# Attention's outputs divided once a pair, with the divisors and the last pair's outputs in slots kept up to the middle of the output projection

## The chip, the cores and the metric

The kernel runs on one core of a Trainium2 chip. The metric is device time in microseconds (us). The core has five engines with queues of their own: PE (TensorE, the matrix multiplier), DVE (VectorE), ACT (ScalarE), POOL (GpSimd) and SP (SyncE, which here only issues DMAs). Each works through its instructions in the order in which they were put, and waits on semaphores for the others. The time before is the median of three runs, 1177.61 us (1175.17 to 1178.79).

## The reference, cut to what matters

One layer of a hybrid block on x of shape (1, 1024, 1024), all in float32: an RMSNorm, one input projection split among three token mixers (causal pooling, gated linear attention, forgetting attention), the output projection of their concatenation with a residual, and a SwiGLU feed-forward with a residual and a last norm. The change is in the forgetting attention, 8 heads of width 64 over 1024 tokens:

```
s = einsum('bhqd,bhkd->bhqk', qb, kh) + Fb[..., None] - F[:, :, None, :]
s = where(kpos <= qpos, s, -inf)
p = softmax(s, axis=-1)
o = einsum('bhqk,bhkd->bhqd', p, vh)
```

The softmax divides each row of exponentials by its sum. Since the product with vh is linear in p, the division of row q may be done on p, ahead of the product, or on row q of o, behind it.

## The kernel before, in words

**Precision.** Matmuls that need float32's accuracy are made of three products of a rounded high part and a low remainder (names end in h and l, or hi and lo); a "split" makes the two parts, the high one by an ACT copy, the low one by a subtraction on DVE or POOL.

**Slots.** Nearly all of SBUF is 33 slots of 128 x 1024 floats plus 17 more in five rings. G(name) takes the first slot of the list idle, free(...) appends slots to its end (lines 50 to 58): first in, first out. A tile that inherits a slot waits until the last reader of the slot's tile before it is done. So which earlier tile a tile inherits from decides when its DMA may start. The rings join the list behind the attention (line 713).

**Order.** The program is written as one stream; a scheduler then fixes each engine's order ahead of the run, on its own model of durations, ahead in the program before later where both are ready. Hence projections that come later in the program fill PE between an attention item's steps.

**Stages.** The first norm, linear attention and pooling come first. Then, for four pairs of heads p (line 680): fox_attend (attention of the pair), fox_qk(p + 1) (the next pair's queries and keys, tiles q, k, kl, from the transposed input hT, the names zq and zk), then keep_mix(4 + p), which splits the pair's output y (tile mh is the high part) and stores both parts by two SP DMAs to a DRAM buffer mixs. For pair 1, fox_values also makes the values v2, v3 of the last two pairs.

fox_attend runs eight items (head a of the pair, group m of 256 queries: lines 634, 635). An item makes for both of its 128-query blocks the scores in PSUM (s, lines 576 to 579), adds the forget bias and takes the row minimum on DVE (line 581), and takes the exponential on ACT with the row sum as accumulated output (line 585). Then it takes the reciprocals of the two sums (line 588), and multiplies the first block's exponentials by them on POOL (line 591) and the second's on DVE (line 593). Blocks of four 128 x 128 tiles are then transposed on PE (pt, line 602), split by ACT and DVE (lines 604, 605), and multiplied with the values into o (line 616), which has one PSUM bank. Lines 619 and 622 add the two halves of o to the 64 output rows of head a: into tile y for pairs 0 to 2; for pair 3, whose order of items is m = 1, 0, 3, 2, into a temporary that is split at once into last_mix (lines 625, 626).

**Output projection.** It runs in two passes over eight token tiles of 128. The first pass (pxa, lines 699 to 708) takes the mixers 0 to 3: weights wo0 to wo3 (each in two slots, from the DRAM buffer wod), the input tile xa, and the mixes of 512 tokens at a time (mix0_g to mix3_g), 24 matmuls of 128x512 a tile. The second pass (pxb, line 935 on) takes mixers 4 to 7, that is the four pairs, with wo4 to wo7, mix4 to mix6 from DRAM and last_mix in place, and is followed a tile at a time by the second norm (norm2) and the first parts of the feed-forward (products named m, line 775).

Of the kernel before, what the change touches and what calls it, by code (L numbers as in the profile page):

```python
# [18 lines left out]
P = 128  # L19
# [12 lines left out]
def tile_hybrid_block(ctx: ExitStack, tc, x, w_fv, w_gv, w_zt, w_o, w_gu, w_down, ln, w_pool, w_a3, chans, b_f, consts, out):  # L32
    nc = tc.nc
    ACT, DVE, POOL, PE, SP = nc.scalar, nc.vector, nc.gpsimd, nc.tensor, nc.sync
# [4 lines left out]
    dpool = ctx.enter_context(tc.tile_pool(name="dp", bufs=1, space=bass.MemoryType.DRAM))  # L39
# [10 lines left out]
    def G(name, dtype=F32):  # L50
        i = idle.pop(0)
        t_ = big.tile([P, 1024], dtype, tag=f"g{i}", name=name)
        where[name] = i
        return t_

    def free(*names):
        for n in names:
            idle.append(where.pop(n))

    def R(name, dtype=F32, tag="p"):  # L60

# [50 lines left out]
    def PS(tag, name):  # L112
        return pst.tile([P, 512], F32, tag=tag, name=name, bufs=BANKS[tag])
# [22 lines left out]
    def half(name, dtype=F32):  # L136
        return rng.tile([P, 512], dtype, tag="tmp", name=name, bufs=2)
# [25 lines left out]
    def names_T(name):  # L163
        return [f"{name}{k}_{c}_{h}" for k in range(4) for c in range(2) for h in range(2)]
# [128 lines left out]
    last_mix = []  # L293
# [253 lines left out]
                    POOL.tensor_copy(t_[a][own[1 - a], csl], f(t_[a][own[a], csl]))  # L547
        return Q, K, KL

    def fox_item(p, a, m, ops, fb, V, Y):  # L550

        Q, K, KL = (t_[a] for t_ in ops)
        nm = f"{p}_{a}_{m}"
        rows = slice(64 * a, 64 * a + 64)
        Pb, Ws = [], []
        l, rl = S(f"l{nm}", 2), S(f"rl{nm}", 2)
        for i in range(2):
            qb = 2 * m + i
            W = P * (qb + 1)
            nh = 1 if W <= 512 else 2  # L560
            w = W // nh
            qs = slice(qb * P, (qb + 1) * P)
            mn = S(f"mn{nm}_{i}")
            if m >= 2:
                pb = R(f"pb{nm}_{i}")
            elif i == 0:
                pb2 = R(f"pb{nm}")
                pb = pb2[:, 0:512]
            else:
                pb = pb2[:, 512:1024]  # L570
            top = 3.0e38
            for h in range(nh):
                s = PS("s", f"s{nm}_{i}_{h}")
                ks = slice(h * w, (h + 1) * w)
                last = h == nh - 1
                PE.matmul(s[:, 0:w], Q[:, qs], K[:, ks], start=True, stop=False)  # L576
                PE.matmul(s[:, 0:w], Q[:, qs], KL[:, ks], start=False, stop=not last)  # L577
                if last:
                    PE.matmul(s[:, w - P:w], identr, maskr, start=False, stop=True)
# [5 lines left out]
            ACT.activation(pb[:, 0:W], pb[:, 0:W], AF.Exp, bias=mn[:, 0:1], scale=-1.0, accum_out=l[:, i:i + 1])  # L585
            Pb.append(pb)
            Ws.append(W)
        DVE.reciprocal(rl, l)  # L588
        for i, (pb, W) in enumerate(zip(Pb, Ws)):
            if i == 0:  # L590
                POOL.tensor_tensor(out=pb[:, 0:W], in0=pb[:, 0:W], in1=rl[:, 0:1].broadcast_to([P, W]), op=ALU.mult)  # L591
            else:
                DVE.tensor_scalar(out=pb[:, 0:W], in0=pb[:, 0:W], scalar1=rl[:, 1:2], scalar2=None, op0=ALU.mult)
        o = PS("o", f"o{nm}")
        for n in range(m + 1):
            pt = PS("pt", f"pt{nm}_{n}")
            pp = R(f"pp{nm}_{n}", F32R, tag="pp")
            cut = P if n == m else 0
            for b in range(2):
                for i in range(b if cut else 0, 2):  # L600
                    o0 = 256 * b + P * i - cut * b
                    PE.transpose(pt[:, o0:o0 + P], Pb[i][:, (2 * n + b) * P:(2 * n + b + 1) * P], ident)  # L602
            w = 512 - cut
            ACT.activation(pp[:, 0:w], pt[:, 0:w], AF.Copy)  # L604
            DVE.tensor_tensor(out=pp[:, 512:512 + w], in0=pt[:, 0:w], in1=f(pp[:, 0:w]), op=ALU.subtract)  # L605
            for b in range(2):
                kb = 2 * n + b
                o0 = cut * b
                v_ = V[p % 2][kb // 4][:, kb % 4, a]
                ph = pp[:, 256 * b:512 - o0] if b else pp[:, 0:256]  # L610
                pl = pp[:, 768:1024 - o0] if b else pp[:, 512:768]
                both = (o[:, o0:256], v_.rearrange("p s e -> p (s e)"), ph)
                high = (o[0:64, o0:256], v_[:, 0], pl)
                last = kb == 2 * m + 1
                for n_, args in enumerate((high, both) if last else (both, high)):
                    PE.matmul(*args, start=(kb == 0 and n_ == 0), stop=(last and n_ == 1))  # L616
        tmp = half(f"ot{nm}")
        ot, oy = tmp[0:64, 0:256], tmp[:, 256:512]
        ACT.activation(ot, o[64:128, 0:256], AF.Copy)
        if p < 3:  # L620
            oy = Y[:, m * 256:(m + 1) * 256]
        DVE.tensor_tensor(out=oy[rows], in0=o[0:64, 0:256], in1=ot, op=ALU.add)
        if p == 3:
            hi, lo = (last_mix[m // 2][rows, h, (m % 2) * 256:(m % 2 + 1) * 256] for h in range(2))
            ACT.activation(hi, oy[rows], AF.Copy)
            POOL.tensor_tensor(out=lo, in0=oy[rows], in1=f(hi), op=ALU.subtract)

    def fox_attend(p, ops, V, Y):
        fbs = []
        for a in range(2):  # L630
            fb = R(f"fb{p}_{a}", tag="fb")
            SP.dma_start(fb, Fd[2 * p + a:2 * p + a + 1, :].broadcast_to([P, T]))
            fbs.append(fb)
        for a, m in ([(a, m) for a in range(2) for m in range(4)] if p < 3 else [(a, m) for m in (1, 0, 3, 2) for a in range(2)]):
            fox_item(p, a, m, ops, fbs[a], V, Y)


    x3d = [dpool.tile([P, D], F32, name=f"x3d{tb}") for tb in range(NT)]
# [36 lines left out]
    V = fox_values(0, (B.within(1), o_[0][:1], o_[0][1:], o_[1][:1], o_[1][1:] + B.turned(0), B.turned(1), (), ()))  # L675
    for k in range(8):
        keep_wo(k)
    ops = fox_qk(0)
    free("gv0", "gv1", "attb0", "attb1")
    for p in range(4):  # L680
        if p == 3:
            last_mix += [G(f"mix7_{g}", F32R).rearrange("p (h t) -> p h t", h=2) for g in range(2)]
        Y = G(f"y{p}") if p < 3 else None
        fox_attend(p, ops, V, Y)
        done = [f"{n}{p}_{a}" for n in ("q", "k", "kl") for a in range(2)] + [f"v{p}_{i}" for i in range(2)]
        if p == 1:
            V = fox_values(1)
            free(*[done.pop() for _ in range(2)])
        if p < 3:
            ops = fox_qk(p + 1)  # L690
        if p == 2:
            free(*names_T("hT"))
        if p < 3:
            free(*done)
            keep_mix(4 + p, Y)
            free(f"y{p}")


    ws = [fetch_wo(k) for k in range(4)]
# [1 line left out]
    for g in range(2):  # L701
# [282 lines left out]
    sums = {}  # L984
# [139 lines left out]
```

## Time and profile before

| what | us |
|---|---|
| median of three runs | 1177.61 |
| lowest, highest | 1175.17, 1178.79 |
| profiled execution: its own time | 1177.97 |
| profiled execution: span of the core | 1176.0 |
| PE busy in the span | 1136.7 |
| DVE, ACT, POOL busy in the span | 823.9, 537.0, 339.7 |
| mean granted TensorE clock | 0.992 |
| last output of pair 0, 1, 2, 3 (start of the sum, line 622) | 300.0, 353.3, 435.5, 495.5 |
| first and last matmul of pxa | 398.1, 469.2 |
| first and last matmul of pxb | 470.5, 533.0 |

Times inside the span count from its start. PE's busy time is modelled from pipelined matmuls, so a stretch in which it is fully busy may still hold short waits. "<-" behind an idle time names what ended it. A row of the grouped views gives line, engine, operation, the tile written and those read, shape, count, then busy us, mean ns of one, and idle us ahead.

### The profile page before, as it was taken

The page shows a single profiled execution, that of the slowest core. Times are in us where ns is not written, and L with a number is a line of the kernel's source. Part 1 is how long each engine was busy: PE and PEld are TensorE (multiplying, and loading weights), DVE is VectorE, ACT ScalarE, POOL GpSimd, SP SyncE. Part 2 cuts the span into 40 slices and gives each one's busy share as a digit, 9 for nine tenths or more (in the row PEclk, how much of TensorE's full clock was granted, in tenths as well). Part 3 has the DMA queues.
Part 4 walks back from the last instruction along what each step waited for, and adds up shares of the span by engine and source line. Part 5 has one row for each costly group of instructions (what it writes and reads, how often), then busy time and mean ns, then how long its engine had stood idle before and what let it go on. Part 6 is the DMA issues. An engine that isn't in the chain of part 4 may idle for free.

```text
span 1176.0 us, 15954 instructions
## 1 busy us (share of the span) xinstructions
PE 1136.7 (97%) x5928; PEld 959.4 (82%) x5928; DVE 823.9 (70%) x1365; ACT 537.0 (46%) x972; POOL 339.7 (29%) x260
## 2 busy tenths in 40 slices
PE   6999998999999999998999999999999999999996
PEld 6877878889978888886888888888888888888885
DVE  7596364287746866579997768777776684976686
ACT  6453344366654644456453434443343344334344
POOL 2131122443322313110202221022202271660693
PEclk9999999999999999999999999999999999999999
DMA  7111179311203734431333232332324688333233
GB/s 250 36 37 37 37 264 351 102 37 37 91 18 122 308 127 158 163 127 37 107 100 134 88 128 69 119 121 95 109 80 152 215 323 291 107 96 105 80 118 143
DMA packets 57692, 150.45 MB, mean 128 GB/s; under 512 B 5080, under 2 KB 5512, under 8 KB 57616
## 3 DMA queue, kind: packets, MB, share of 16 engines
q1 hardware_dynamic: 57184, 147.87, 36.8%
q0 software_dynamic: 432, 1.57, 0.4%
q8 instruction: 46, 0.75, 0.3%
q14 instruction: 30, 0.25, 0.1%
HBM read 105.09 MB, written 44.34 MB: 127 GB/s over the span
## 4 chain that ended last, share of the span: by engine, by line
PE 81%; DVE 7%; DMA 5%; POOL 3%; issue 2%; ACT 1%; SPq 0%; POOLq 0%; ACTq 0%; DVEq 0%
PE m L775 35%; PE d L1031 13%; PE pxa L144 4%; PE pxb L144 3%; PE o L616 3%; PE psv L152 2%; PE pt L602 2%; POOL rw L873 2%; PE s L576 1%; PE s L577 1%; PE zq3p L152 1%; PE psg L144 1%; PE zgk1p L152 1%; PE zgg0p L152 1%; PE zq2p L152 1%
## 5 line engine op out<-in xcount | busy, mean ns | idle before, releaser
L775 PE MATMUL m<-hA_0h,wr 128*128 128x512 f32 x616 | 214.2, 391 | 0.9 <-ACT hr L730 0.9
L775 PE MATMUL m<-hA_1h,wr 128*128 128x512 f32 x616 | 214.6, 389 | 0.0
L775 PEld LDWEIGHTS m<-hA_0h,wr 128*128 128x128 f32 x616 | 116.0, 188 | 25.3 <-ACT hr L730 1.4
L775 PEld LDWEIGHTS m<-hA_1h,wr 128*128 128x128 f32 x616 | 115.7, 188 | 23.9
L757 ACT ACTIVATE wr<-ws 128x512 fp32r<-128x512 f32 x110 | 69.2, 631 | 120.6 <-DVE ws L756 61.9
L775 PE MATMUL m<-hA_0l,wr 128*128 128x512 f32 x308 | 120.2, 390 | 0.7 <-DVE hA_0l L905 0.7
L1031 PE MATMUL d<-lw,ha 128*128 128x512 f32 x308 | 119.8, 389 | 0.0
L775 PE MATMUL m<-hA_1l,wr 128*128 128x512 f32 x308 | 119.8, 389 | 0.0
L1031 PE MATMUL d<-hw,ha 128*128 128x512 f32 x308 | 119.3, 389 | 0.0
L1031 PE MATMUL d<-hw,la 128*128 128x512 f32 x308 | 118.4, 389 | 0.0
L827 POOL TENSOR_TENSOR cg<-cu,cu 128x512 f32<-128x512 f32 x11 | 19.7, 1793 | 304.9 <-DVE cu L804 268.6
L758 DVE TENSOR_TENSOR wr<-ws,wr 128x512 fp32r<-128x512 f32 x110 | 75.6, 694 | 26.9 <-ACT wr L757 26.8
L881 DVE TENSOR_TENSOR la<-ra,ha 128x1024 fp32r<-128x1024 f32 (+1 forms) x42 | 57.5, 1375 | 30.1 <-ACT ha L880 22.4
L873 POOL TENSOR_TENSOR rw<-wd,wd 128x512 f32<-128x512 f32 x33 | 59.6, 1833 | 48.0 <-PE d L1031 47.9
L591 POOL TENSOR_TENSOR pb<-pb,rl 128x128 f32<-128x128 f32 (+3 forms) x32 | 39.3, 1232 | 115.2 <-DVE rl L588 105.1
L880 ACT ACTIVATE ha<-ra 128x1024 fp32r<-128x1024 f32 (+1 forms) x42 | 41.2, 987 | 65.6 <-DMA ra<-cd 60.6
L775 PEld LDWEIGHTS m<-hA_0l,wr 128*128 128x128 f32 x308 | 58.0, 188 | 13.2 <-DVE hA_0l L905 1.1
L585 ACT ACTIVATE pb<-pb,mn 128x128 f32<-128x128 f32 (+3 forms) x64 | 49.5, 774 | 41.1 <-DVE mn L581 39.8
L605 DVE TENSOR_TENSOR pp<-pt,pp 128x512 fp32r<-128x512 f32 (+1 forms) x80 | 50.1, 631 | 25.7 <-ACT pp L604 25.5
L775 PEld LDWEIGHTS m<-hA_1l,wr 128*128 128x128 f32 x308 | 57.8, 188 | 12.1
L1031 PEld LDWEIGHTS d<-hw,ha 128*128 128x128 f32 x308 | 57.8, 188 | 12.1
L1031 PEld LDWEIGHTS d<-hw,la 128*128 128x128 f32 x308 | 57.8, 188 | 12.1
(399 smaller groups left out, 2699.1 us busy)
## 6 DMA issues: line engine op xcount, KB each, us to landing
ra<-cd SPq DMA_DIRECT2D x35, 512.0 KB, 3.9
wu<-in_w_gu_dram SPq DMA_DIRECT2D x22, 512.0 KB, 4.8
wg<-in_w_gu_dram SPq DMA_DIRECT2D x22, 512.0 KB, 3.7
wd<-in_w_down_dram SPq DMA_DIRECT2D x22, 512.0 KB, 6.7
mix<-mixs SPq DMA_DIRECT2D x14, 512.0 KB, 6.1
cd<-cg SPq DMA_DIRECT2D x11, 512.0 KB, 6.4
cd<-cs SPq DMA_DIRECT2D x11, 512.0 KB, 3.4
cd<-cu SPq DMA_DIRECT2D x11, 512.0 KB, 3.4
```

Of the source, the lines that this page charges most:

```text
L144: PE.matmul(ps, a, b, start=(n == 0), stop=(n == last))
L152: PE.matmul(ps, a, b, start=(i == 0 and n == 0), stop=(i == len(terms) - 1 and n == 2))
L585: ACT.activation(pb[:, 0:W], pb[:, 0:W], AF.Exp, bias=mn[:, 0:1], scale=-1.0, accum_out=l[:, i:i + 1])
L591: POOL.tensor_tensor(out=pb[:, 0:W], in0=pb[:, 0:W], in1=rl[:, 0:1].broadcast_to([P, W]), op=ALU.mult)
L605: DVE.tensor_tensor(out=pp[:, 512:512 + w], in0=pt[:, 0:w], in1=f(pp[:, 0:w]), op=ALU.subtract)
L757: ACT.activation(hi, src, AF.Copy)
L758: DVE.tensor_tensor(out=lo, in0=src, in1=f(hi), op=ALU.subtract)
L775: PE.matmul(ps, a, b, start=(n == 0), stop=(n == 11))
L873: POOL.tensor_tensor(out=raw_[:, j * 512:j * 512 + 512], in0=wd[h0, j0 + j][:, e0, :], in1=wd[h1, j0 + j][:, e1, :], op=op)
L880: ACT.activation(hi[:, sl], src, AF.Copy)
L881: DVE.tensor_tensor(out=lo[:, sl], in0=src, in1=f(hi[:, sl]), op=ALU.subtract)
L1031: PE.matmul(banks[t], a[:, o], b[:, ns], start=(j0 + j == 0 and m == 0), stop=(j0 + j == NF // 2 - 1 and m == 2))
```

## The change

The multiplications on the exponentials and the reciprocal of each item go away: an item now works on undivided exponentials, and ACT puts each row sum into one column of a tile of 16 columns for the pair. The new function divide(p, Y, sums, g) works on half g of the tokens (512), for both heads: it takes the reciprocals of 8 columns, transposes them on PE into 8 rows, copies these out of PSUM, writes them to a DRAM buffer Ld, reads them back twice as a broadcast over 64 partitions (one for each head), and multiplies Y by the result on POOL. All three DMAs are issued by POOL.

For pairs 0 to 2 both halves are divided behind fox_qk(p + 1), ahead of keep_mix. For pair 3 the first half is divided behind its fourth item and the second behind its last, and divide makes the split into last_mix for the half. So pair 3 now has a tile y3 as well. Each divide takes a slot rb. Those of pairs 0 to 2 are freed with y behind keep_mix; y3, rb3_0 and rb3_1 are freed behind the first pass of the output projection.

```diff
-        l, rl = S(f"l{nm}", 2), S(f"rl{nm}", 2)
...
-            ACT.activation(pb[:, 0:W], pb[:, 0:W], AF.Exp, bias=mn[:, 0:1], scale=-1.0, accum_out=l[:, i:i + 1])
+            ACT.activation(pb[:, 0:W], pb[:, 0:W], AF.Exp, bias=mn[:, 0:1], scale=-1.0, accum_out=sums[:, col(a, qb)])
...
-        DVE.reciprocal(rl, l)
-        for i, (pb, W) in enumerate(zip(Pb, Ws)):
-            if i == 0:
-                POOL.tensor_tensor(out=pb[:, 0:W], in0=pb[:, 0:W], in1=rl[:, 0:1].broadcast_to([P, W]), op=ALU.mult)
-            else:
-                DVE.tensor_scalar(out=pb[:, 0:W], in0=pb[:, 0:W], scalar1=rl[:, 1:2], scalar2=None, op0=ALU.mult)
...
-        if p < 3:
-            oy = Y[:, m * 256:(m + 1) * 256]
-        DVE.tensor_tensor(out=oy[rows], in0=o[0:64, 0:256], in1=ot, op=ALU.add)
+        DVE.tensor_tensor(out=Y[rows, m * 256:(m + 1) * 256], in0=o[0:64, 0:256], in1=ot, op=ALU.add)
+    Ld = dpool.tile([4, 2, 2, 512], F32, name="Ld")
+    def col(a, qb):
+        c = 8 * (qb // 4) + 4 * a + qb % 4
+        return slice(c, c + 1)
+    def divide(p, Y, sums, g):
+        nm = f"{p}_{g}"
+        rw = G(f"rb{nm}")
+        rl, rt, rb, gs = S(f"rl{nm}", 8), rw[0:8, 512:640], rw[:, 0:512], slice(g * 512, g * 512 + 512)
+        DVE.reciprocal(rl, sums[:, 8 * g:8 * g + 8])
+        pt = PS("pt", f"ptl{nm}")
+        PE.transpose(pt[0:8, 0:P], rl, ident)
+        ACT.activation(rt, pt[0:8, 0:P], AF.Copy)
+        POOL.dma_start(Ld[p, g].rearrange("a (q t) -> (a q) t", t=P), rt)
+        for a in range(2):
+            POOL.dma_start(rb[64 * a:64 * a + 64, :], Ld[p, g, a:a + 1, :].broadcast_to([64, 512]))
+        POOL.tensor_tensor(out=Y[:, gs], in0=Y[:, gs], in1=rb, op=ALU.mult)
         if p == 3:
-            hi, lo = (last_mix[m // 2][rows, h, (m % 2) * 256:(m % 2 + 1) * 256] for h in range(2))
-            ACT.activation(hi, oy[rows], AF.Copy)
-            POOL.tensor_tensor(out=lo, in0=oy[rows], in1=f(hi), op=ALU.subtract)
+            ACT.activation(last_mix[g][:, 0], Y[:, gs], AF.Copy)
+            POOL.tensor_tensor(out=last_mix[g][:, 1], in0=Y[:, gs], in1=f(last_mix[g][:, 0]), op=ALU.subtract)
...
-            fox_item(p, a, m, ops, fbs[a], V, Y)
+            fox_item(p, a, m, ops, fbs[a], V, Y, sums)
+            if p == 3 and (a, m) == (1, 0):
+                divide(p, Y, sums, 0)
+        if p == 3:
+            divide(p, Y, sums, 1)
...
-        Y = G(f"y{p}") if p < 3 else None
+        Y = G(f"y{p}")
...
+            for g in range(2):
+                divide(p, Y, sums, g)
             keep_mix(4 + p, Y)
-            free(f"y{p}")
+            free(f"y{p}", f"rb{p}_0", f"rb{p}_1")
...
-    free(*[f"wo{k}{h}" for k in range(4) for h in "hl"], *done)
+    free(*[f"wo{k}{h}" for k in range(4) for h in "hl"], *done, "y3", "rb3_0", "rb3_1")
```

More of the change, by code (lines that the diff above doesn't have):

```diff
@@ L548, in fox_qk, with fox_item @@
         return Q, K, KL
-    def fox_item(p, a, m, ops, fb, V, Y):
+    def fox_item(p, a, m, ops, fb, V, Y, sums):
         Q, K, KL = (t_[a] for t_ in ops)
@@ L554, in fox_item @@
         rows = slice(64 * a, 64 * a + 64)
-        Pb, Ws = [], []
-        l, rl = S(f"l{nm}", 2), S(f"rl{nm}", 2)
+        Pb = []
         for i in range(2):
@@ L583, in fox_item @@
                 top = t_[:, 0:1]
-            ACT.activation(pb[:, 0:W], pb[:, 0:W], AF.Exp, bias=mn[:, 0:1], scale=-1.0, accum_out=l[:, i:i + 1])
+            ACT.activation(pb[:, 0:W], pb[:, 0:W], AF.Exp, bias=mn[:, 0:1], scale=-1.0, accum_out=sums[:, col(a, qb)])
             Pb.append(pb)
-            Ws.append(W)
-        DVE.reciprocal(rl, l)
-        for i, (pb, W) in enumerate(zip(Pb, Ws)):
-            if i == 0:
-                POOL.tensor_tensor(out=pb[:, 0:W], in0=pb[:, 0:W], in1=rl[:, 0:1].broadcast_to([P, W]), op=ALU.mult)
-            else:
-                DVE.tensor_scalar(out=pb[:, 0:W], in0=pb[:, 0:W], scalar1=rl[:, 1:2], scalar2=None, op0=ALU.mult)
         o = PS("o", f"o{nm}")
@@ L616, in fox_item @@
                     PE.matmul(*args, start=(kb == 0 and n_ == 0), stop=(last and n_ == 1))
-        tmp = half(f"ot{nm}")
-        ot, oy = tmp[0:64, 0:256], tmp[:, 256:512]
+        ot = half(f"ot{nm}")[0:64, 0:256]
         ACT.activation(ot, o[64:128, 0:256], AF.Copy)
-        if p < 3:
-            oy = Y[:, m * 256:(m + 1) * 256]
-        DVE.tensor_tensor(out=oy[rows], in0=o[0:64, 0:256], in1=ot, op=ALU.add)
+        DVE.tensor_tensor(out=Y[rows, m * 256:(m + 1) * 256], in0=o[0:64, 0:256], in1=ot, op=ALU.add)
[15 more added lines that the diff above has]
+        POOL.tensor_tensor(out=Y[:, gs], in0=Y[:, gs], in1=rb, op=ALU.mult)
         if p == 3:
-            hi, lo = (last_mix[m // 2][rows, h, (m % 2) * 256:(m % 2 + 1) * 256] for h in range(2))
-            ACT.activation(hi, oy[rows], AF.Copy)
-            POOL.tensor_tensor(out=lo, in0=oy[rows], in1=f(hi), op=ALU.subtract)
+            ACT.activation(last_mix[g][:, 0], Y[:, gs], AF.Copy)
+            POOL.tensor_tensor(out=last_mix[g][:, 1], in0=Y[:, gs], in1=f(last_mix[g][:, 0]), op=ALU.subtract)
     def fox_attend(p, ops, V, Y):
@@ L633, in fox_attend @@
             fbs.append(fb)
+        sums = S(f"l{p}", 16)
         for a, m in ([(a, m) for a in range(2) for m in range(4)] if p < 3 else [(a, m) for m in (1, 0, 3, 2) for a in range(2)]):
-            fox_item(p, a, m, ops, fbs[a], V, Y)
+            fox_item(p, a, m, ops, fbs[a], V, Y, sums)
[3 more added lines that the diff above has]
+            divide(p, Y, sums, 1)
+        return sums
     x3d = [dpool.tile([P, D], F32, name=f"x3d{tb}") for tb in range(NT)]
@@ L682, in tile_hybrid_block @@
             last_mix += [G(f"mix7_{g}", F32R).rearrange("p (h t) -> p h t", h=2) for g in range(2)]
-        Y = G(f"y{p}") if p < 3 else None
-        fox_attend(p, ops, V, Y)
+        Y = G(f"y{p}")
+        sums = fox_attend(p, ops, V, Y)
         done = [f"{n}{p}_{a}" for n in ("q", "k", "kl") for a in range(2)] + [f"v{p}_{i}" for i in range(2)]
```

## The prediction

> **What bounds the kernel now.** I read the page first: its busy times and the chain of work that ended last.
>
> ```profile
> PE 1136.7 (97%) x5928; PEld 959.4 (82%) x5928; DVE 823.9 (70%) x1365; ACT 537.0 (46%) x972; POOL 339.7 (29%) x260
> PE 81%; DVE 7%; DMA 5%; POOL 3%; issue 2%; ACT 1%; SPq 0%; POOLq 0%; ACTq 0%; DVEq 0%
> ```
>
> TensorE sets the time; what the change removes runs on DVE and POOL. So the next view is busy time by stretch: attention and the first half of the output projection as a whole (225 to 500 us), and places in and after it. Columns: stretch and its length, then busy us of PE, PEld, DVE, ACT, POOL, then the granted clock, DMA share, GB/s.
>
> ```profile
> 225.00:500.00 275.00, 269.95 (x1646) 238.60 (x1645) 182.66 (x439) 146.62 (x314) 83.92 (x83) 0.99 0.33 116
> ...
> 340.00:360.00 20.00, 16.76 (x87) 13.69 (x86) 8.70 (x14) 7.54 (x13) 7.53 (x8) 0.91 0.13 52
> 380.00:400.00 20.00, 19.26 (x123) 16.66 (x122) 16.56 (x48) 13.40 (x30) 9.55 (x12) 1.00 1.03 390
> 460.00:480.00 20.00, 18.98 (x116) 16.44 (x115) 9.97 (x21) 7.93 (x17) 3.98 (x5) 1.00 0.53 185
> ```
>
> Of 275 us PE idles 275 - 269.95 = 5.05 us, and the clock of 0.99 costs about 2.75 us more. **A lighter attention can win at most these 7.8 us.** The projections of the next pair and, from 398 us, the output projection fill PE while an attention item waits for its softmax. The largest hole is at 346 to 354 us, between pair 1 and pair 2, and the chain shows what is in it.
>
> ```profile
> 350.96 0.99 PE o L616 x7
> 351.98 0.69 DVE kl L545
> 352.69 0.60 ACT k L544
> 353.30 0.41 DVE y L622
> 353.74 0.70 DVE kl L545
> 354.49 6.43 PE zq3p L152 x20
> ```
>
> The last item of pair 1 has run out of filler (pair 2's projection zk2 has been multiplied, its PSUM is not yet emptied), and the evictions of zk2 stand in DVE's and ACT's order among that item's own work. Multiplications by the divisor don't appear on that path; only their being gone from the items ahead can pull the item forward.
>
> **Part 1: what goes.** Grouped by line, within 225 to 500 us:
>
> ```profile
> L591 POOL TENSOR_TENSOR pb<-pb,rl 128x128 f32<-128x128 f32 (+3 forms) x32 | 39.3, 1232 | 115.2 <-DVE rl L588 105.1 <-PE pt L602 8.3 <-PE zk3p L152 0.9
> L593 DVE TENSOR_SCALAR pb<-pb,rl 128x256 f32<-128x256 f32 (+3 forms) x32 | 27.1, 848 | 0.8
> L588 DVE RECIPROCAL rl<-l 128x2 f32<-128x2 f32 x32 | 5.2, 162 | 9.3 <-ACT pb L585 9.1
> ```
>
> 32 reciprocals and 64 multiplications: 39.3 us of POOL and 32.3 us of DVE, hidden under PE today. Per item about 0.16 + 1.23 us leave the way from the exponential to the first transpose. On the path this can only fill holes. I take -4 us, most of the hole at 346 us (3.24 us idle there, plus 0.09 x 20 = 1.8 us of clock); bounds 0 (the planner only moves filler about) and -7.8.
>
> **Part 2: what is added.** Eight divides (two halves of four pairs). Each has a PE transpose and its eviction, three POOL DMAs in a row (a write to DRAM, then two reads that wait for it), and one POOL multiplication of 128x512; for pair 3 the split moves from eight 64-row pieces to two of 128 rows. The rows near these steps, each from the view of its tile or from the DMA issues (the last two numbers are KB each and us to landing):
>
> ```profile
> L715 POOL DMA_DIRECT2D ln2b<-in_ln_dram x1: 647/647/647, 467.5 to 467.5; - x1
> DMA to landing us min/median/max: 7.5/7.5/7.5
> ```
>
> ```profile
> cd<-cu SPq DMA_DIRECT2D x11, 256.0 KB, 2.1
> mixs<-y SPq DMA_DIRECT2D x3, 512.0 KB, 3.6
> ```
>
> ```profile
> L994 POOL TENSOR_TENSOR c<-c,lnfb x8: 1292/1811/2277, 1110.4 to 1156.3; 128x512 f32<-128x512 f32 x8
> ```
>
> The 288 transposes of the items are the nearest row for the eight new ones:
>
> ```profile
> L602 PE MATMUL pt<-ident,pb 128*128 128x128 f32 x288 | 44.7, 274 | 0.0
> ```
>
> On PE itself they cost 8 x 44.7 / 288 = +1.2 us (bounds 0, in a hole, and 8 x 0.274 = 2.2). For the latency of one divide: reciprocal 0.16, transpose and eviction about 0.7, then DMAs that no row shows at this size. From below the 2.1 us row, from above the 7.5 us row, for each of the two serial legs; I take 3.6 for each (neither leg is large), plus three issues of 0.65, plus the multiplication 1.8: 0.16 + 0.7 + 7.2 + 2.0 + 1.8, about 12 us (bounds 9 and 20). The Trainium skill ("DMA: Bandwidth & Descriptors", Anatomy of one DMA) gives a DMA issued from GpSimd a fixed cost of about 2.0 us plus bytes over 436 GB/s, most of it completion. By it the legs would be 2.0 and 2.3 us (an estimate from that page), a divide about 9 us, and the sum below would shrink by at most 1 us in the term for the second half; no run yet shows a DMA of this size.
>
> For pairs 0, 1 and the first half of pair 3 nobody waits for those 12 us: the mixes go out to DRAM and come back after 440 us, or are used there. The second half of pair 3 is used by token tile 4 of the second projection (pxb), after 4 tiles of 24 matmuls. A tile is one piece of the chain:
>
> ```profile
> 500.50 5.50 PE pxb L144 x24
> ```
>
> So 4 x 5.50 = 22 us after pxb starts, against a divide of 12 us: that is the cover, and were it gone, the cost would be what the divide exceeds it by.
>
> **Part 3: what moves, the slots.** The slots are a first-in-first-out list, so each added one shifts who inherits what. I replayed the list by hand with rb and y3 in it. Before, wo0 to wo3, the first half's mixes and xa0 inherit hT, free when zk3 is multiplied (387.5 us); wo4h, wo4l and wo5h inherit mixes of the first half, so they are fetched early; mix4_0, mix5_0 and mix6_0 inherit k3_0, k3_1 and kl3_0, free when pair 3's scores are done. After, mix1_0 and mix3_0 inherit q2_1 and k2_1 (pair 2's last scores); xa2 and xa3 inherit v2 (pair 2's end); mix0_1 to mix3_1 inherit mh6, y2 and rb2, free only behind pair 2's divides and its store; **all eight wo4 to wo7 inherit mix0_1 to mix3_1 and wo0h to wo1l, free only as the first projection ends; mix5_0 and mix6_0 inherit v3, free only when attention ends.** The DMA issues and the first and last starts of the tiles show what such inheritances cost:
>
> ```profile
> 431.28 0.33 SPq L290 DMA_DIRECT2D wo4h<-wod  x1
> ...
> 463.95 0.52 SPq L648 DMA_DIRECT2D mix<-mixs  x1
> 467.42 0.33 SPq L290 DMA_DIRECT2D wo5l<-wod  x1
> 467.80 0.43 SPq L290 DMA_DIRECT2D wo7l<-wod  x1
> 468.34 0.36 SPq L290 DMA_DIRECT2D wo6h<-wod  x1
> ...
> 469.98 0.33 SPq L290 DMA_DIRECT2D wo7h<-wod  x1
> ...
> 495.05 0.53 SPq L648 DMA_DIRECT2D mix<-mixs  x1
> ```
>
> ```profile
> L144 PE MATMUL pxa<-wo3h,mix x32: 387/389/452, 404.8 to 469.2; 128*128 128x512 f32 x32
> ```
>
> ```profile
> L144 PE MATMUL pxb<-wo6h,mix x32: 387/389/499, 476.8 to 532.4; 128*128 128x512 f32 x32
> ```
>
> ```profile
> L144 PE MATMUL pxb<-wo7h,mix x32: 388/389/397, 480.1 to 533.0; 128*128 128x512 f32 x32
> ```
>
> ```profile
> L622 DVE TENSOR_TENSOR y<-o,ot x24: 404/417/419, 252.1 to 435.5; 64x256 f32<-64x256 f32 x24
> L622 DVE TENSOR_TENSOR ot<-o,ot x8: 406/417/418, 443.3 to 495.5; 64x256 f32<-64x256 f32 x8
> ```
>
> Already before, the last five wo loads are issued at 467.4 to 470.0, as the first projection (pxa) ends at 469.2; wo6h is multiplied first at 476.8 and wo7h at 480.1. That hole is filled by what is left of attention, which ends at 495.5: PE idles only 20 - 18.98 = 1.02 us there. After, this cover is thin from both sides. Attention comes ahead of pxa in the program and its items are shorter, so more of it will be done when pxa ends; and if some is left, mix5_0 and mix6_0 wait behind it.
>
> Gap between the projections: six loads with ln2b took 467.4 to 480.1, some 12.7 us; taking 5.5 us for the first, (12.7 - 5.5) / 5 = 1.4 us for each further one; nine take 5.5 + 8 x 1.4 = 16.7 us, from 2.2 us ahead of pxa's end: 14.5 us after it. Until then PE can multiply k = 4 to 6 of one token tile, 36 x 5.50 / 24 = 8.2 us, as pairs land. Idle 14.5 - 8.2 = 6.3 us if both halves of the tile are taken, 10.4 us if one. I take 7, less the 1 us idle today: **+6 us** (bounds +3, one 512 KB transfer of 3.6 us behind the last of the two and little else, and +13).
>
> The clock behind that gap: the stretch with 3.24 us idle shows 0.91, so +1.8 us (bounds 0 and 1.8).
>
> Start of pxa:
>
> ```profile
> 387.56 10.41 DMA mix<-mixs
> ```
>
> ```profile
> 399.98 0.33 SPq L632 DMA_DIRECT2D fb<-Fd  x1
> ```
>
> Pair 3's second fb load at 399.98 shows that pair 2's last scores are just done then; mix1_0 and mix3_0 can't be loaded before, and land some 5 us later (3.6 to 7.5 by the rows above), against pxa's start now, when the load of 387.56 is in at 387.56 + 10.41 = 397.97. Pair 2's items fill PE meanwhile, though not tightly (0.74 us idle in 380 to 400): +2 us (bounds 0 and 6).
>
> Second half of pxa: pair 2 ends at 435.5 before; with a divide of 12 us, the split, a store of 3.6 and a load of 3.6 to 6, mix0_1 and mix1_1 arrive at 455 to 460 or, with pair 2 done 5 us sooner, near 452. Tile 4 of pxa is the middle of its stretch (398 to 469.2), at 434 now, some us later as the items take their share. Pair 3 fills PE for these 10 to 18 us, which is the very filler that is missing later; by itself +1 us (bounds 0 and 10).
>
> **Sum** against the profiled execution (span 1176.0 us, its time 1177.97, the median of the runs 1177.61, so 0.4 us under it): -4 + 1.2 + 6 + 1.8 + 2 + 1 = +8.0 us, 1186.0, on the median 1185.6. I say **1186 us**.
>
> **Rivals.** (a) The shorter items win. Attention needs some 32 us less of DVE; if the planner keeps enough of pair 3 for the gap and the holes close, it is -7.8 + 1.2 + 3 (the least gap, net of what idles there today) = about -4 us: 1174. For it speaks the POOL row, where 105.1 us were spent waiting for reciprocals; against it, PE at 269.95 of 275. It decides where attention and pxa end within 4 us of each other. (b) No change, 1178: the holes at 346 us close (-4) and the gap costs the least. (c) A larger loss: pxa's second half waits for pair 2's divides with pair 3 used up, +10 there, and the gap at its +13: -4 + 1.2 + 13 + 1.8 + 2 + 10 = +24, less some 4 us that the two stalls share: 1198. It decides from a divide of 15 us or more. (d) The change doesn't shorten anything, because the items wait for PE and not for the divisor; then -4 becomes 0, 1190, inside my range.
>
> **How the numbers follow.** Forecast with (d): 0.50; (c) 0.19; (b) 0.16; (a) 0.15. A run of this kernel is told from no change at 0.3%, 3.5 us. The forecast's own range, 1182 to 1192, is slower throughout, as is (c). So slower 0.69, same 0.16, faster 0.15. The range 1173.5 to 1199 holds 8 of 10 cases: its lower end cuts (a) in the middle, its upper end leaves out the worse half of (c).
>
> **What would show it.** Right: all eight wo4 to wo7 loads issued within 4 us of pxa's end, PE idle for 5 us or more between pxa and pxb with the waits naming a wo or mix load, attention over before pxb's wo6h, mix loads of the second half behind pair 2's store, a lower clock in that stretch, and fewer idle us at 340 to 360. Wrong: PE never idle there, or wo4h still fetched 30 us ahead of pxb (the slots then run otherwise than I replayed); PE waiting at a divide's transpose; or a stall of POOL's key copies (L547) behind a divide's DMA wait, which would move a whole pair.

## The result, and the profile after

The changed kernel takes **1207.75 us** (median of four runs, 1206.97 to 1208.97) against 1177.80 in runs of the kernel before made beside it: slower, ratio 1.026, 95% interval 1.0248 to 1.028. That is +30 us where +8 was forecast, and above the range's upper end of 1199. The profiled execution has a span of 1207.2 us, 31.2 more than before.

The page of the changed kernel: busy times, and the shares of the chain that ended last.

```profile
PE 1148.1 (95%) x5936; PEld 965.5 (80%) x5936; DVE 795.8 (66%) x1309; ACT 536.3 (44%) x974; POOL 318.7 (26%) x254
PE 77%; DMA 9%; DVE 6%; POOL 3%; issue 3%; ACT 1%; SPq 0%; POOLq 0%; ACTq 0%; DVEq 0%
```

DVE and POOL did lose the work that was taken from them (28 and 21 us). The chain shows who set the time in their place: DMA's share went from 5% to 9% of the span, some 50 us more. The stretches say where; their columns are those of the prediction's table. First the kernel before over the whole region, then the changed kernel over it and in places.

```profile
225.00:520.00 295.00, 289.95 (x1748) 255.46 (x1747) 197.11 (x457) 157.30 (x335) 85.94 (x87) 0.99 0.34 117
```

```profile
225.00:520.00 295.00, 270.37 (x1596) 235.33 (x1595) 150.86 (x378) 139.28 (x305) 60.17 (x72) 0.95 0.34 113
340.00:360.00 20.00, 17.56 (x95) 14.95 (x94) 5.86 (x10) 6.39 (x13) 9.04 (x14) 0.91 0.00 0
...
400.00:420.00 20.00, 17.58 (x89) 14.84 (x88) 9.88 (x27) 7.93 (x19) 0.00 (x0) 0.83 0.31 106
440.00:460.00 20.00, 16.27 (x93) 13.91 (x92) 13.23 (x35) 11.16 (x23) 4.19 (x5) 0.83 0.80 253
460.00:480.00 20.00, 16.65 (x96) 14.10 (x95) 7.06 (x15) 5.44 (x12) 3.60 (x4) 1.00 0.39 116
480.00:500.00 20.00, 16.06 (x92) 13.75 (x90) 8.12 (x14) 3.81 (x9) 2.18 (x4) 1.00 0.28 92
500.00:520.00 20.00, 13.46 (x43) 9.04 (x44) 2.69 (x4) 1.78 (x3) 3.28 (x4) 0.74 0.79 290
```

PE's idle time in the region went from 295 - 289.95 = 5.05 to 24.63 us, +19.6; the clock of 0.95 in place of 0.99 costs at most 295 x 0.04, about 12 us more, if PE had work all the time. The whole span agrees: by the pages' busy times PE idles 59.1 us in place of 39.3, +19.8, and its busy time grows by 11.4, which is mostly the lower clock, since it has only 8 matmuls more. All but a remnant of the loss lies in five stretches: 400 to 420 (2.42 us idle, and 0.17 x 20 = 3.4 of clock), 440 to 480 (3.73 + 3.35 idle, 3.4 of clock) and 480 to 520 (3.94 + 6.54 idle, 5.2 of clock). PE's waits in the region (in all, times, longest):

```profile
PE pxa L144 <- DMA mix<-mixs: 6.5, 4, 2.4
PE pxb L144 <- DMA wo4h<-wod: 4.9, 1, 4.9
PE pxb L144 <- DMA wo5h<-wod: 2.8, 1, 2.8
PE pt L594 <- ACT rb L628: 2.7, 1, 2.7
PE zq3p L152 <- DVE kl L545: 2.4, 1, 2.4
PE pxb L144 <- DMA mix<-mixs: 1.8, 1, 1.8
```

Of these only the fifth was there before at this size. The other five are, in order of place: the first projection pxa waiting for its mixes (at 406, and again up to 463 and 468 us), an attention item waiting for a divide's eviction (453 us), and the second projection pxb waiting for its weights and a mix.

**Between the projections.** The order of issue on SP's queue, then the chain there, then the rows of the tiles.

```profile
493.42 0.33 SPq L290 DMA_DIRECT2D wo6l<-wod  x1
...
497.45 0.53 SPq L290 DMA_DIRECT2D wo7l<-wod  x1
```

```profile
493.42 5.04 DMA wo6l<-wod
...
498.52 14.36 DMA mix<-mixs
512.88 0.04 issue
512.93 7.08 PE pxb L144 x30
```

```profile
L144 PE MATMUL pxa<-wo3h,mix x32: 389/390/628, 409.0 to 495.3; 128*128 128x512 f32 x32
```

```profile
L144 PE MATMUL pxb<-wo6h,mix x32: 389/389/499, 512.9 to 563.1; 128*128 128x512 f32 x32
```

```profile
L611 DVE TENSOR_TENSOR y<-o,ot x32: 406/417/419, 243.6 to 497.0; 64x256 f32<-64x256 f32 x32
```

All eight wo4 to wo7 are issued between 493.42 and 497.45, as pxa ends at 495.3: the slots run as they were replayed. Behind them a mix load needs 14.36 us. And attention's last output is at 497.0, against 495.5 before, while pxa's last matmul moved from 469.2 to 495.3. Before, pair 3 filled PE for 26 us behind pxa's end; this **lead** is now 1.7 us, and almost nothing is left to fill the gap.

**Behind pair 2.** The chain through its two divides:

```profile
435.81 4.22 DMA rb<-Ld
...
440.20 1.29 POOL y L632
...
442.24 8.13 DMA rb<-Ld
...
450.54 1.26 POOL y L632
...
454.17 7.13 DMA mixs<-y
461.30 0.02 issue
461.32 6.90 DMA mix<-mixs
468.22 0.04 issue
468.26 1.88 PE pxa L144 x7
```

The mix that pxa waits for at 468 holds none of pair 2's output (pxa takes mixers 0 to 3). By the replay of the slots it waits for the slot of y2 alone: two divides, a store of 7.13 and only then its own load of 6.90.

### The profile page after: what moved, and what is told of

Same layout as the page of the kernel before. It is cut to its first block, busy times and chain, and to the rows that moved or that the text cites. A ratio compares the mean times of both kernels' runs of the same rounds, so it can differ in the third digit from the quotient of the medians.

```text
span 1207.2 us, 15873 instructions
## 1 busy us (share of the span) xinstructions
PE 1148.1 (95%) x5936; PEld 965.5 (80%) x5936; DVE 795.8 (66%) x1309; ACT 536.3 (44%) x974; POOL 318.7 (26%) x254
## 4 chain that ended last, share of the span: by engine, by line
PE 77%; DMA 9%; DVE 6%; POOL 3%; issue 3%; ACT 1%; SPq 0%; POOLq 0%; ACTq 0%; DVEq 0%
PE m L792 34%; PE d L1048 12%; PE pxa L144 3%; PE pxb L144 3%; DMA mix<-mixs 3%; PE o L608 2%; PE psv L152 2%; PE pt L594 2%; DMA rb<-Ld 2%; POOL rw L890 2%; PE zq3p L152 1%; PE psg L144 1%; PE zgk1p L152 1%; PE s L575 1%; PE zgg1p L152 1%
## 5 line engine op out<-in xcount | busy, mean ns | idle before, releaser
L1048 PEld LDWEIGHTS d<-lw,ha 128*128 128x128 f32 x308 | 57.8, 188 | 11.9
L596 ACT ACTIVATE pp<-pt 128x512 fp32r<-128x512 f32 (+1 forms) x80 | 43.1, 553 | 53.2 <-PE pt L594 45.8
```

The source lines that it names most:

```text
L1048: PE.matmul(banks[t], a[:, o], b[:, ns], start=(j0 + j == 0 and m == 0), stop=(j0 + j == NF // 2 - 1 and m == 2))
```

## The experiments

Ratios are to the kernel before on the same chip. "Without slots" means that the broadcast divisors of pairs 0 to 2 lie in the tile mh of keep_mix (made just ahead of the divides), and that y3 and pair 3's divisors lie in ring tiles; the slot list then runs as before.

| kernel | median us | ratio | 95% interval |
|---|---|---|---|
| changed kernel | 1207.75 | 1.0264 | 1.0248 to 1.0280 |
| 1 divides, no slots | 1184.24 | 1.0074 | 1.0054 to 1.0094 |
| 2 slots alone | 1189.95 | 1.0123 | 1.0102 to 1.0144 |
| 3 the last three slots alone | 1192.21 | 1.0136 | 1.0105 to 1.0167 |
| 4 rb of pairs 0 to 2 alone | 1178.63 | 1.0029 | 1.0013 to 1.0046 |
| 5 divide without DMA, no slots | 1184.47 | 1.0072 | 1.0052 to 1.0093 |
| 6 divide without DMA, with slots | 1198.84 | 1.0200 | 1.0173 to 1.0227 |
| 7 no division at all | 1175.84 | 1.0004 | 0.9990 to 1.0017 |
| 8 last three in rings | 1198.31 | 1.0202 | 1.0169 to 1.0235 |
| 9 no slots, pair 3 only | 1174.56 | 0.9972 | 0.9962 to 0.9983 |
| 10 no slots, pairs 0 to 2 only | 1182.23 | 1.0039 | 1.0023 to 1.0056 |
| 11 one divide a pair | 1202.53 | 1.0209 | 1.0191 to 1.0227 |
| 12 pair 3 only, rest as before | 1183.43 | 1.0059 | 1.0041 to 1.0077 |

The theory from the traces: most of the loss comes from the slots, the rest from the divide's length under them. The rival: the divides themselves, wherever their tiles lie.

**1, 2: the divide and the slots apart.**

```diff
 # 1: the changed kernel
-        rw = G(f"rb{nm}")
+        rb = f(mh[:, gs]) if p < 3 else R(f"rb{nm}", tag="w")[:, 0:512]
...
-        Y = G(f"y{p}")
+        Y = G(f"y{p}") if p < 3 else R("y3", tag="w")
 # 2: the kernel before; reserve(n) takes a slot and puts nothing in it
+                reserve(f"rb{p}_{g}")
+            for n in ("y3", "rb3_0", "rb3_1"):
+                reserve(n)
```

> The changed kernel's arithmetic and its divides with all their DMAs, but no slot of the list: rb of pairs 0 to 2 lies in the tile mh of keep_mix, y3 and both rb3 lie in the ring of weights that is idle by then, so that every slot is inherited as before. Theory S (the changed order of inheritance costs the 30 us): 1172 to 1181 us, wo4h fetched near 431 again. Theory D (the divides' DMA round trips cost it): 1190 us or more, with PE waiting behind rb.

> The kernel before, arithmetic untouched, in which rb0_0 to rb3_1 and y3 are only taken from the list and given back where the change does it; nothing is read or written there. Theory S: most of the loss is back, 1195 to 1205 us, all eight wo loads issued as the first projection ends; what is missing from 1207.8 is what mix0_1 to mix3_1 wait for a divide. Theory D: within 5 us of before, 1178 to 1183.

The divides without slots cost 7.8 us, empty slots 13.5: the slots weigh more, and both are real. Neither kernel lies where a theory put it: the first falls between the two (1181 and 1190), the second between 1183 and 1195, so neither theory holds alone. The two costs add up to 21.3 of the 30 us. In the second kernel the hole ahead of pxb stands by itself, without one divide in the program. One stretch of it, and a wait:

```profile
480.00:500.00 20.00, 13.92 (x48) 11.44 (x49) 2.96 (x5) 2.30 (x5) 0.72 (x1) 0.66 0.62 235
```

```profile
PE pxb L147 <- DMA mix<-mixs: 6.0, 1, 6.0
```

6.1 us idle and a clock of 0.66 in 20 us. Attention's last output comes at 485.5 there and pxa's last matmul at 474.9: a lead of 10.6 us where 26.3 were. In the first kernel the loss begins much earlier, at pair 0. Its chain:

```profile
296.63 5.13 DMA mh<-Ld
...
303.82 2.91 DMA mh<-Ld
...
308.20 1.07 ACT mh L274
...
309.29 0.61 DVE y L275
...
311.50 0.29 DVE v L531
...
311.83 6.40 PE zq2p L152 x20
```

PE waits there 2.3 us for the eviction of a projection's PSUM tile (v, line 531), which has nothing to do with the divide. It stands behind keep_mix's split (ACT line 274, DVE line 275) in two queues fixed ahead of the run, and the split waits for two DMA legs. Only a part of the 7.8 us lies there. About 3 us lie far behind it, in 520 to 560 us, where the second norm waits for DVE: PE idles 6.50 us there in place of 5.04, and the clock is 0.91 in place of 0.96.

**3, 4: which slots.**

```diff
 # 3: the kernel before, reserving y3, rb3_0 and rb3_1 only
+            for n in ("y3", "rb3_0", "rb3_1"):
+                reserve(n)
 # 4: the kernel before, reserving the six rb of pairs 0 to 2 only
+                reserve(f"rb{p}_{g}")
```

> The kernel before with only y3, rb3_0 and rb3_1 taken from the list and given back behind the first projection, empty. By the replayed list all eight wo4 to wo7 and mix5_0, mix6_0 then inherit late slots, as in the changed kernel. If the gap between the projections is what the slots cost: 1186 to 1191 us, nearly all of the 13.5 us that all reservations cost. If the loss comes from mix0_1 to mix3_1 and the start of the first projection: 1177 to 1181.

> The kernel before with only rb0_0 to rb2_1 taken and given back, empty: wo4 to wo7 and mix4 to mix6 inherit exactly as before. If the gap is what the slots cost: within 3 us of before, 1174 to 1180. Otherwise 1183 or more.

The three slots kept to the end of pxa cost all of it (16.8 us, a little over the 1191 that was expected at most, against 13.5 for all nine; the two intervals overlap). The six others, empty, cost 3.2. The leads go with that: 8.1 us in the third kernel (486.0 and 477.9), 19.4 in the fourth (490.6 and 471.2).

**5, 6: the divide without its DMAs.**

```diff
+        DVE.tensor_copy(wide.rearrange("p (q a e) -> p a q e", q=4, a=2), rl.rearrange("p (a q e) -> p a q e", a=2, e=1).broadcast_to([P, 2, 4, 64]))
+        for q in range(4):
+            PE.transpose(pt[:, q * P:(q + 1) * P], wide[:, q * P:(q + 1) * P], ident)
+        DVE.tensor_tensor(out=Yg, in0=pt, in1=Yg, op=ALU.mult)
-        POOL.dma_start(...)   three times, and POOL's multiplication
```

> As the first kernel, but the divide uses no DMA: the reciprocals are spread by DVE over 512 columns, transposed by four PE transposes into one PSUM bank, and DVE multiplies y by that. Theory S: within 3 us of the first kernel. Theory D: faster than the first kernel by 10 us or more, back at 1178 or under.

> The changed kernel with its slots taken and freed as there, but the divides without DMAs as in the kernel before this one. Theory S: 1193 to 1203 us; the gap between the two projections stays, and only the wait of mix0_1 to mix3_1 for pair 2's divides shrinks by some 10 us. Theory D: 1176 to 1184.

Without slots the DMA legs make no difference (8.0 against 7.8 us; that what is saved in waiting goes into the four transposes and two passes of DVE a divide is argued). With the slots they do: 22.4 against 30 us. So a divide's length costs time where slots hang on it.

**7: what the removal is worth.**

```diff
-        DVE.reciprocal(rl, l)
-        for i, (pb, W) in enumerate(zip(Pb, Ws)):
-            ...
```

> The kernel before without the 32 reciprocals and 64 multiplications and with nothing in their place; the softmax isn't divided, so this part of the computation is left out. It shows what shorter items are worth at most. By the prediction's term: -4 us, 1172 (bounds 1168 to 1177). By the reading that the two kernels without slots, 8 us above before, suggest (the scheduler lays filler otherwise and new holes open): 1177 to 1186.

In all, nothing: 1.0004, interval 0.9990 to 1.0017. The hole at 340 to 360 is as large as before (PE busy 16.77 in place of 16.76):

```profile
340.00:360.00 20.00, 16.77 (x89) 13.84 (x88) 8.23 (x17) 8.41 (x18) 7.52 (x8) 0.91 0.21 79
```

The items did get shorter all the same. Attention's last output comes at 483.9 us in place of 495.5, and in 225 to 520 us PE idles 3.26 us in place of 5.05. The gain is lost behind that, where the second norm waits for DVE (PE's longest wait there is 5.8 us, 3.5 before), and over the whole span PE idles 39.1 us, 39.3 before. Two stretches, first of the kernel before, then of this one:

```profile
520.00:540.00 20.00, 18.02 (x87) 14.51 (x85) 18.00 (x26) 14.82 (x34) 4.80 (x6) 1.00 0.20 80
540.00:560.00 20.00, 16.93 (x70) 13.67 (x71) 19.86 (x33) 12.43 (x24) 0.00 (x0) 0.91 0.14 33
```

```profile
520.00:540.00 20.00, 13.89 (x70) 11.18 (x68) 16.83 (x26) 12.16 (x28) 2.42 (x4) 0.92 0.13 53
540.00:560.00 20.00, 20.00 (x82) 16.39 (x82) 19.48 (x33) 13.06 (x23) 0.00 (x0) 0.91 0.32 94
```

**8: the last three slots mended.**

```diff
-        rw = G(f"rb{nm}")
+        rw = G(f"rb{nm}") if p < 3 else R(f"rb{nm}", tag="w")
...
-    free(..., *done, "y3", "rb3_0", "rb3_1")
+    free(..., *done)
```

> The changed kernel with one part undone: y3, rb3_0 and rb3_1 lie in the weights' ring that is idle by then, rb of pairs 0 to 2 stay in the list. If the last pair's three slots make the gap: no idle of 5 us between the projections, 1185 to 1195 us. If the divides' DMA chain is what costs beside the 8 us of the arithmetic: 1198 or more.

The first reading missed, and the time is just at the 1198 of the second: 23 us of the loss stay. wo4h, wo4l and wo5h are fetched early again (432 to 435 us, as before), the others at 488 to 491, and the gap is still open, since the lead is gone here too (last output 487.8, pxa's last matmul 490.2). The loss sits one step earlier now. PE's largest wait, and two stretches:

```profile
PE pt L594 <- DVE pp L597: 5.5, 2, 4.9
```

```profile
440.00:460.00 20.00, 14.92 (x91) 13.44 (x89) 12.71 (x33) 11.06 (x24) 5.14 (x7) 0.83 0.69 210
...
480.00:500.00 20.00, 13.78 (x69) 10.70 (x67) 5.12 (x9) 2.12 (x5) 2.25 (x5) 0.94 0.56 179
```

That wait of 4.9 us is for the eviction of an item's transposes: it stood on ACT and DVE behind pair 2's split, which itself waited for POOL's multiplication (ACT's part of the split starts at 451.4, DVE's at 452.5). So the two parts of the loss aren't a sum of their own: the late weights alone open the gap (third kernel), and the long divides in the list alone use up what would fill it (eighth).

**9, 10: where the 8 us without slots lie.**

```diff
 # 9: kernel 1, the divides of pairs 0 to 2 left out
-            for g in range(2):
-                divide(p, Y, sums, g, mh)
 # 10: kernel 1, pair 3 not divided (line "if p < 3:" ahead of divide's work)
```

> The divide without slots, for pair 3 alone: pairs 0 to 2 are left undivided, which is left out of the computation. With all four pairs divided that way the kernel took 1184.2 us, 8 more than before. Theory: those 8 us come from pairs 0 to 2, where DVE's and ACT's queues stand behind a split that waits for the divide: then 1176 to 1179 here, and the profile has no wait of 2.3 us at 311 us. Rival: they come from pair 3's divide, on which the second projection waits, and from the DVE-bound stretch at 540 to 560 us: then 1181 to 1185.

> The divide without slots, for pairs 0 to 2 alone: pair 3 is left undivided, which is left out of the computation. Theory (the cost is the queues behind the splits of pairs 0 to 2): 1181 to 1185, with PE waits of 2 us and more at about 312 us and about 350 us. Rival (the cost is pair 3's divide): 1176 to 1179. If it and the kernel that divides pair 3 alone both stand near 1180, the 8 us have two places.

The divides of pairs 0 to 2 cost 4 to 5 us by themselves (tenth kernel). Of the two waits that were expected, the one at 312 is there, 2.2 us, and its chain is that of the first kernel; the hole at 340 to 360 is hardly larger than before (PE busy 16.41 in place of 16.76). Pair 3's divides alone cost nothing; that kernel is 0.3% under the one before, lower than either reading put it. What wins the 3 us isn't shown: with nothing divided at all the seventh kernel stood at 1.0004. But the parts don't add: -3 and +4.5 against +8 together, so the theory holds for where the cost of pairs 0 to 2 arises and not for the whole.

**11: one divide for both halves.**

```diff
+    def divide_pair(p, Y, sums):
+        rb, other = G(f"rb{p}_0"), G(f"rb{p}_1")
+        rl, rt = S(f"rl{p}", 16), other[0:16, 0:128]
...
-            for g in range(2):
-                divide(p, Y, sums, g)
+            divide_pair(p, Y, sums)
```

> The changed kernel, with one divide for both halves of pairs 0 to 2 (one transpose of 16 columns, one write of 8 KB, two reads of 128 KB broadcast to 64 partitions, two multiplications); pair 3 and every slot as in the changed kernel. Theory (the mixes of the second half come late because two divides stand one behind the other on POOL, 20 us in all): pair 2's last multiplication ends about 8 us sooner, at 443 to 446 us in place of 451.8, the wait of pxa for a mix at about 465 us is gone or under 1 us, and the time is 1197 to 1203. Rival (the order of the slots alone holds the loads, the divide's length is covered): 1205 to 1209, with the same waits.

(Its reads are of 256 KB each, not 128 as said above.) In its chain the store and the load behind pair 2, and the stretch around them:

```profile
443.61 6.66 DMA mixs<-mh
450.29 4.72 DMA mix<-mixs
455.05 2.92 PE pxa L144 x6
```

```profile
440.00:460.00 20.00, 12.56 (x55) 10.87 (x54) 9.29 (x24) 8.36 (x18) 4.56 (x6) 0.68 0.80 263
```

The last multiplication of pair 2 ends at 442.4 in place of 451.8, and the mix in the slot of mh is in at 455.0 in place of 463.5. (The one in y2's slot, in at 468.2 there, is no longer waited for.) The kernel gains only 5 us on the changed one, and the wait for a mix is still there, 3.6 us at its longest, where under 1 us was expected. Of the 7.4 us idle in this stretch the rest is one wait of 3.8 us at 441 to 445, at the transpose of pair 3's first divide, for the eviction of an item's tile (DVE pp); the clock is 0.68. So the serial divides are part of the loss, and the forecast that their end would close the wait was wrong. That the fixed order put less other work ahead of it is a reading, not tested.

**12: a version that might win.** Pair 3 divided behind, the others on their exponentials as before.

```diff
-        DVE.reciprocal(rl, l)
+        if p < 3:
+            DVE.reciprocal(rl, l)
...
+            if p == 3 and (a, m) == (1, 0):
+                divide(p, Y, sums, 0)
```

> The kernel before, with the divide (no slots) in place of the multiplications on the exponentials for pair 3 alone; pairs 0 to 2 as before, so the whole computation is there. Theory: pair 3's mixes are used from on-chip memory and no store, load or split of 1024 columns stands behind its divide, eight 64-row splits become two, so the divide costs nothing and may win a little: 1173 to 1176, the first kernel of this study under the one before. Rival: the 0.3% seen with pairs 0 to 2 undivided came from the exponentials of those pairs being left alone: then 1177 to 1180, no difference or a little slower.

It doesn't: 1.0059, slower even than the rival expected. Two stretches:

```profile
460.00:480.00 20.00, 16.98 (x90) 14.37 (x88) 7.08 (x18) 5.14 (x10) 3.17 (x3) 0.91 0.53 179
...
540.00:560.00 20.00, 14.03 (x53) 10.89 (x54) 19.30 (x32) 12.02 (x26) 1.68 (x2) 0.83 0.16 53
```

3.0 us idle at the start of pxb, in a wait for wo5l (1.02 before), and 6 us where DVE is nearly full behind it (3.1 before, PE busy 16.93). Why the same divide of pair 3 wins 3 us in the ninth kernel and loses 7 here isn't settled; the two differ in pairs 0 to 2 alone, and in the ninth attention's last output comes at 488.1, here at 499.3. None of the kernels run beats the one before with its whole computation.

## Why the prediction was wrong, step by step

The direction and the places were right, and every sign that was named for "right" is in the trace: the eight loads within 4 us of pxa's end, waits of pxb for a wo and a mix, attention over before wo6h, the mix loads behind pair 2's store, the lower clock. Of the signs named for "wrong", PE waiting at a divide's transpose and an early wo4h are not there. Term by term, forecast against trace:

| term | forecast (bounds) | trace |
|---|---|---|
| shorter items | -4 (-7.8 to 0) | -0.8 at 340 to 360; in all 0 by the seventh kernel |
| start of pxa | +2 (0 to 6) | +5.8, its clock with it |
| second half of pxa | +1 (0 to 10) | +10.5, its clock with it |
| gap between the projections | +6 (+3 to +13) | +9.5 (10.48 idle, 1.02 before) |
| clock behind the gap | +1.8 (0 to 1.8) | +5.2 |

With the 1.2 that was put for the transposes (forecast, not measured) the right column makes 31.4 against 31.2 measured. That it closes so well is in part luck: the clock's share is taken as if PE had been busy throughout, but in 501.1 to 511.4, at a clock of 0.50, PE was busy for 6.20 of 10.3 us, so there about 3.1 of the 5.2 us were lost to the clock and the rest counts twice.

**The step that failed is the cover of the stalls, and with it the clock.** The prediction let other work hide most of each stall, and of the clock that stalls cost it priced only the gap's, at one portion of 1.8 us. Taken apart:

| part | forecast | trace |
|---|---|---|
| idle at the start of pxa, in its second half, in the gap | 2 + 1 + 6 = 9 | 2.4 + 7.1 + 9.5 = 19.0 |
| clock of the same three | 0 + 0 + 1.8 | 3.4 + 3.4 + 5.2 = 12.0 at most |

The worst single term is the second half of pxa: "Pair 3 fills PE for these 10 to 18 us", so +1, where PE idled 7.1 us. An item's transposes waited 2.7 us there behind a divide's eviction, and pxa 1.2 and 2.2 us for mixes. At the last of these waits, from 466.1 to 468.26, three of pair 3's eight items still had transposes and products to do: their last exponentials were done at 463.5, and their outputs come at 480.3, 486.6 and 497.0. So filler wasn't short there; it stood behind pxa's matmuls in PE's fixed order. Work covers a stall only if it stands ahead of the instruction that stalls.

What pair 3 did fill there was then missing behind pxa, where the lead was 1.7 us. The prediction saw this ("the very filler that is missing later") and took 7 us for the gap all the same, near the lower of its two figures (6.3 and 10.4). That the stalls draw on one stock of filler fits the leads of the kernels above; no run tests it by itself. Where rival (c) did add the upper bounds, it took 4 us off for what the stalls share; the trace shows no such saving.

At 406 us the mix was loaded when the prediction said (issued at about 400, landed at 406.1) and the idle 2.4 us are its +2; only the clock was missing there. (pxa begins at 392.4, ahead of the 398.1 before, and stalls inside.)

**Attention ends earlier: wrong for this kernel.** "Its items are shorter, so more of it will be done when pxa ends": the lead did vanish, but in the changed kernel the last output came 1.5 us later than before; it is pxa that came 26 us later. The premise itself holds: with nothing divided (seventh kernel) the last output comes 11.6 us sooner. With all the divides it doesn't, in the list (497.0) or without slots (498.0). With empty slots alone it came 10 us sooner too (second and third kernels), though no item was shorter there; PE worked on the items earlier, and its waits in pxa were only 2.2 and 0.4 us, so it looks like another order of the scheduler's.

**The divide's 12 us.** One multiplication took less than forecast, a DMA leg about what was forecast. Two lines of the view of the tile rb (24 DMAs, 8 writes and 16 reads):

```profile
L632 POOL TENSOR_TENSOR y<-y,rb x8: 1252/1282/1288, 296.0 to 506.8; 128x512 f32<-128x512 f32 x8
...
DMA to landing us min/median/max: 1.6/3.9/8.1
```

What was missed is that pair 2's two divides run one behind the other on POOL's queue (pair 1's don't: both writes start at 354.4, both multiplications are over at 365): from the first eviction at 432.0 to 451.8 it is 20 us, not 12, and the store and the load behind them took 7.13 and 6.90 where 3.6 and 3.6 to 6 were put. So the mix landed at 468, not at 455 to 460. By the Trainium skill ("DMA: Bandwidth & Descriptors", Anatomy of one DMA) a read of 128 KB would take about 2.3 us, an estimate from its 2.0 us and 436 GB/s; this trace doesn't agree: its 16 reads took 3.9 us in the median, and the longest 8.1, while all queues together moved 253 GB/s (440 to 460 us).

**What no step had:** the engines' queues behind the divide. The prediction asked who waits for the divide's result, and found nobody for pairs 0 and 1. But keep_mix's split waits for it, on ACT and DVE, and with it all that was put behind the split: the eviction v at 311 us (first kernel), the items' pp (eighth kernel, 5.5 us), and a divide's own eviction, which held the PSUM buffer that an item wanted (2.7 us in the changed kernel). It named such a stall for POOL's key copies only. That the costs without slots (+8) are such stalls is shown for pair 0 alone, by the chain above. About 3 us of them lie in the second norm instead, and why isn't settled: the kernel with nothing divided loses there too.

**Rival (d)**, the change shortens nothing, holds for the total by the seventh kernel, but not for its reason: attention did end sooner there, and the gain went into the second norm's wait for DVE. Rival (c), put at 1198 with 0.19, was nearest, and still 10 us short.

## What to carry to other kernels

A tile that is kept in a first-in-first-out list of buffers is paid for by whoever inherits next, even where it has none of its data: three empty reservations cost 17 us here, twice what all eight divides cost without slots. Where queues are fixed ahead of the run, spare work hides a stall only if it stands ahead of the stalled instruction: look for it there before a stall is priced near nothing, and price each stall that is left with its clock. And for every operation that waits on a DMA, list what stands behind it on its engine's queue, not only who reads its result.

## What the runs showed of the hardware

The clock is lost in portions. Over stretches of 20 us the granted clock in most rows above takes the values 1.00, 0.91, 0.83, 0.74 and 0.66, steps of about 0.085, that is 1.7 us of lost time each (others, such as 0.94, may be a portion cut by the stretch's edge). How many portions a hole costs is not read from its length: 2.42 us idle at 400 to 420 cost two, 3.35 at 460 to 480 none, the several waits between 496.1 and 512.9 three, where the prediction had one. Windows of 1 us show what a portion is: the granted clock is 0.50 in each from 406 to 412 (0.78 and 0.81 in the two beside them), and from 502 to 511 (0.57 and 0.81 beside them). That is half speed for about 6.8 and 10.2 us, two and three times 3.4, and each 3.4 us at half speed lose 1.7. The Trainium skill ("TensorE: Matmul & The Clock Gate", Part 1) says that the clock falls to half for at least a window of about 3.4 us after an idle window; half of 3.4 is the 1.7 of the steps, so the rows agree with its size. They don't agree that an idle window of 3.4 us is needed: at 400 to 420 PE idled for 2.42 us in all, and the clock fell before that wait was over.

The eight weight loads and the mix behind them, 512 KB each, share what there is: the first landed 5.04 us after its issue, the mix issued last 14.36 us after its own, so (512.88 - 498.46) / 8 = 1.8 us for each further one, where 1.4 had been taken from six loads before. In both cases the load of ln2b, 512 KB too, ran among them and isn't counted.
